# One written-out list of steps for the middle of a decoder block: from the second half of the memory values to the first column group of the up projection

## The chip, the cores and the metric

The kernel runs on one core of one Trainium2 chip. The metric is the device time of one execution in microseconds (us); the runs' median is given. The core has a matrix engine (PE, with its weight loads shown as PEld), a vector engine (DVE), an activation engine (ACT), a general engine (POOL, which also issues DMAs of the software queue) and a sync engine (SP, which here issues plain DMAs). Each engine works through its own instructions in their order and waits for others by semaphores. Matrix products are added up in banks of PSUM and read from there by ACT and DVE.

## The reference, cut to what matters

A decoder block for 1024 tokens of width 1024, all in 32-bit floats. The part that the change touches is everything between the memory attention's softmax and the up projection:

```python
def _memory_cross_attention(h, m, w_q, w_kv, w_o):
    ...
    o = jnp.einsum('bhqk,bhkd->bhqd', p.astype(v.dtype), v)
    return jnp.einsum('bsc,cd->bsd', _merge(o), w_o)
    ...
    x = x + jnp.einsum('bsc,cd->bsd', mixed, w_out[l])
    h = _rmsnorm(x, xattn_norm_g[l])
    m = _rmsnorm(mem, mem_norm_g[l])
    x = x + _memory_cross_attention(h, m, w_mq[l], w_mkv[l], w_mo[l])
    h = _rmsnorm(x, ffn_norm_g[l])
    u = jnp.einsum('bsd,df->bsf', h, w_up[l])
    u = _causal_dwconv(u, conv_w[l], conv_b[l])
    gate, val = jnp.split(u, 2, axis=-1)
    x = x + jnp.einsum('bsf,fd->bsd', jax.nn.silu(gate) * val, w_down[l])
```

Ahead of it stand two kinds of causal self-attention over 8 heads each; behind it the down projection and a last norm. d_ff is 2816, so the up projection has 22 column groups of 128 gate and 128 value columns.

## The kernel before, in words

**Numbers as pairs.** An operand of a product is a pair of a rounded high part and a low part. ACT (sometimes POOL) rounds the high part, DVE subtracts it from the source to get the low part (`split` L204, `split_op` L1127). `mm3` (L199) then makes three matmuls of 128 x 512 for each product of a 128-row tile: high x high (L201), high x low (L202), low x high (L203).

**Products from seven parts.** The memory's output projection ("mo") and the up projection are each computed from 2 x 2 blocks with seven products in place of eight, from sums of blocks. So many sums of operands have to be ready, and each product's result is added to several places. Product 1 of mo is the loop over `pmo` (L1086 to L1103): its first half goes, negated, into `u` (ACT, L1099) and out of the residual `xr` (DVE, L1101). Then come five products by `mo_product` (L1135) in the order 5, 7, 6, 3, 4, each of 4 steps f with 2 splits and 4 x 3 matmuls, which end in 4 banks that `done5` to `done4` (L1150 to L1167) add to `xr` or `u` by DVE. `xr` are 8 tiles of 128 tokens x 1024 columns.

**Sums of the doubled operands.** The second half of the memory values is copied by ACT to `s1` and `s3` and to `a22` and `a22n12` (`evac1`, L1067). The sums that mo's products want are then made by accumulating DMAs of POOL's queue (`onto_a`, L1073): s1 += a22; s3 += high and low of the first half; later s1 += high and low again and s3 += s4. `u` goes into `xr` by 12 more accumulating DMAs of 256 KB, 4 ahead of product 5 and 8 behind product 6 (L1100, L1161). The operand differences of the weights are made by DVE (b11 = b12 - b11, L1115; b22 - b11, L1123) and POOL (b12 - b22, L1116; b21 - b11, L1182).

**Norm and first columns.** `ffn_norm` (L1203) normalises 4 tiles at a time; PE transposes them (`tr`, L1214, bank `ptn`), and `f1` and the pair `b` come from that (L1228 to L1233). For the second 4 tiles the loop at L1347 makes the pairs t1, b22, t2, t3, t4 (tiles `t`, `bt_q`, `bt_k`, `bt_v`). Weights of a column group n are loaded as raw tiles, and `prep_gate`, `prep_sums` and `prep_a22` make its seven operands a11, a12, s1 to s4, a22 (POOL sums L1284 to L1290, splits by ACT or POOL and DVE). Products p1 and p2 of n = 0 and 1 come first, then p5, p6, p7 of column 0 k by k with p4 one behind, then p3 and p4. The loop over the other columns follows, each 7 products of 4 x 3 matmuls, with `cg` and `cv` as sums, the convolution (`conv`, L1386) and the gate. One tile `cg` serves all columns: `first_sum` (L1330) writes it for the next column once the convolution of the last has read it.

**What sets the order.** The two self-attentions and the mixed projection's first half are ordered by `Plan` (L53): a list of `Step`s, each with an engine, a length in ns, the steps that it comes after, named buffers that it takes and gives back, a due time `at`, a time `late` until others see its end, and `lock` (DVE and POOL slow each other while both are in such a step). `run` simulates the engines and returns the steps in their order; they are emitted with the framework's own scheduling switched off. All that follows the mixed projection, the stage of the change included, is ordered by the framework's scheduler. In both cases the framework puts in the waits by what the instructions read and write. The pool `wk` has 4 tiles of 128 x 1024 for normalised rows, softmax rows and operands.

Of the kernel before, what the change touches and what calls it, by code (L numbers as in the profile page):

```python
# [19 lines left out]
P = 128  # L20
D = 1024
# [31 lines left out]
class Plan:  # L53
# [3 lines left out]
    def __init__(self, bufs):  # L57
        self.bufs, self.steps, self.emitted = dict(bufs), [], 0
# [21 lines left out]
    def run(self):  # L80
# [13 lines left out]
        while len(order) < len(left):  # L94
# [39 lines left out]
def hybrid_block(ctx, tc, x, mem, w, wf, pcol, bfg, fing, out):  # L134
# [816 lines left out]
    wk = mid.enter_context(tc.tile_pool(name="wk", bufs=4, reuse_waits="tile"))  # L951
# [67 lines left out]
    def mem_values(probs, evac):  # L1019
        for h in range(4):  # L1020
            pth, ptl = [], []
            for mb in range(2):
                pt = ps.tile([P, 512], F32, tag="T", name="ptm", bufs=2)
                for j in range(4):
                    T.transpose(pt[:, j * P:(j + 1) * P],
                                probs[h][:, j, mb * P:(mb + 1) * P], ident)
                if mb == 0:
                    t = sqp.tile([P, 1024], F32R, tag="sq", name="ptm0")
                    a_, b_ = t[:, :512], t[:, 512:]
                else:  # L1030
                    a_ = wrk.tile([P, 512], F32R, tag="pth1", name="pthm")
                    b_ = wrk.tile([P, 512], F32R, tag="ptl1", name="ptlm")
                split(a_, b_, pt, 1.0)
                pth.append(a_)
                ptl.append(b_)
            for cc in range(2):
                c = 2 * h + cc
                po = ps.tile([P, 512], F32, tag="P", name="pom", bufs=3)
                for mb in range(2):
                    mm3(po, (mv[0][:, mb, c * P:(c + 1) * P], mv[1][:, mb, c * P:(c + 1) * P]),  # L1040
                        (pth[mb], ptl[mb]), mb == 0, mb == 1)
                evac(c, po)
# [7 lines left out]

    probs = mem_probs(0)
    omw = [slot(k, f"om0{n_}").rearrange("p k c -> p (k c)") for k, n_ in ((3, "h"), (0, "l"))]
    om = [[t[:, c * 512:(c + 1) * 512] for c in range(KC)] for t in omw]
    mem_values(probs, lambda c, po: split(om[0][c], om[1][c], po, -1.0))
    probs = mem_probs(1)
    to = ti0 + 8

# [4 lines left out]
    s1t, a22t = [[qkp["f"].tile([P, D], F32, tag=g, name=f"om1{g}{i}") for i in range(2)] for g in ("q", "k1")]  # L1062
    s3t, s4t = [vp.tile([P, 2, 1024], F32, tag="v", name=f"mos{i}") for i in range(2)]
    s3t, s4t = [[t[:, i, :] for i in range(2)] for t in (s3t, s4t)]
    s1, a22, s3, a22n12 = two(s1t), two(a22t), two(s3t), two(s4t)

    def evac1(c, po):  # L1067
        for t in ((s1, s3), (a22, a22n12))[c // 4]:
            A.activation(t[c % 4], po, AF.Copy)

    mem_values(probs, evac1)

    def onto_a(dst, src):  # L1073
        nc.gpsimd.dma_start(dst, src, accum_op=add)

# [4 lines left out]
    for i in range(2):  # L1080
        onto_a(s1t[i], a22t[i])
    for a in range(2):
        for i in range(2):
            onto_a(s3t[i], om_pair(a, 0, i))
    for a in range(2):
        for i in range(2):  # L1086
            onto_a(s4t[i], om_pair(a, 1, i))
    u = vp.tile([P, 2, 1024], F32, tag="v", name="mou")
# [586 lines left out]
```

## Time and profile before

| | us |
|---|---|
| median of 3 runs | 1630.74 |
| lowest and highest run | 1629.62, 1633.43 |
| the profiled execution's own time | 1631.46 |
| its span in the trace | 1629.6 |
| the stage from the second memory values to the end of column group 1 | 177.75 (from 842.00 to 1019.75) |

Rows of windows have: stretch and its length, busy time of PE, PEld, DVE, ACT and POOL with the number of instructions, the clock granted to PE as a share of full speed, the DMA engines' busy share, and GB/s. Rows of groups have: line, engine, operation, output <- inputs, shapes, count | busy time, mean ns of one | idle time of the engine just before. Rows of waits have: who waits <- for what: total, times, longest. Rows of a timeline have: start, time, engine, line and operation, and in brackets the idle time before with what ended it. Rows of DMA issues have: KB of each and median time from issue to landing. A matmul's record is longer than its share of the pace, since matmuls are pipelined.

### The profile page before, as it was taken

To read this page: it belongs to the slowest core of one execution; us is meant where nothing else is said; L and a number is where in the kernel's file an instruction comes from. 1 tells how busy PE (TensorE), PEld (TensorE's weight loads), DVE (VectorE), ACT (ScalarE), POOL (GpSimd) and SP (SyncE) were. 2 spreads that over 40 slices of the span, in tenths; PEclk is the share of its full clock that TensorE was granted. 3 is DMA by queue.
4 is the path that set the end of the run, shared out by engine and by line. 5 is a ranking of instruction groups with operands and counts; after the bars stand their busy time and mean duration, and the time that the engine had idled before them with its cause. 6 is when DMAs were issued, how large, how long until landed. Compare 5 with 4: busy or idle time off the path is not lost. (4 is left out here: it accounts for less than half of the span.)

```text
span 1629.6 us, 22061 instructions
## 1 busy us (share of the span) xinstructions
PE 1547.3 (95%) x7812; PEld 1275.9 (78%) x7812; DVE 1201.1 (74%) x1952; ACT 788.4 (48%) x1546; POOL 540.0 (33%) x534
## 2 busy tenths in 40 slices
PE   7999999999999889999998987999999999999997
PEld 7678887887788767778886765877888888788886
DVE  7377777777867773365544979999999999786566
ACT  7368767767757660034334374333333333445444
POOL 2022313322321210123124439454554444133331
PEclk9999999999999999999999998999999999999999
DMA  5211021011113645512149731222222221998782
GB/s 178 104 53 66 27 65 65 27 53 65 40 53 130 233 142 188 174 45 73 52 139 209 134 119 52 94 87 80 89 78 83 86 91 65 323 296 204 150 189 104
DMA packets 76205, 183.53 MB, mean 113 GB/s; under 512 B 8376, under 2 KB 8504, under 8 KB 75840
## 3 DMA queue, kind: packets, MB, share of 16 engines
q1 hardware_dynamic: 61392, 151.58, 27.1%
q0 software_dynamic: 14400, 30.42, 10.3%
q8 instruction: 61, 1.00, 0.3%
q14 instruction: 48, 0.39, 0.1%
q10 hardware_dynamic: 304, 0.14, 0.0%
HBM read 129.64 MB, written 33.59 MB: 100 GB/s over the span
## 5 line engine op out<-in xcount | busy, mean ns | idle before, releaser
L658 POOL TENSOR_TENSOR p<-p,aw 128x383 f32<-128x383 f32 (+4 forms) x64 | 79.7, 1247 | 182.9 <-DVE aw L652 144.7
L708 DVE TENSOR_TENSOR ptl<-pt,pth 128x512 fp32r<-128x512 f32 x192 | 103.8, 549 | 36.4 <-ACT pth L704 35.0
L202 PE MATMUL dn<-opb,opa 128*128 128x512 f32 x308 | 120.5, 391 | 3.0 <-DVE opb L1133 3.0
L704 ACT ACTIVATE pth<-pt 128x512 fp32r<-128x512 f32 x192 | 92.5, 491 | 60.9 <-PE pt L700 56.9
L203 PE MATMUL dn<-opb,opa 128*128 128x512 f32 x308 | 120.3, 391 | 0.0
L636 POOL TENSOR_SCALAR p<-p,fx 128x128 f32<-128x128 f32 (+3 forms) x64 | 47.9, 753 | 212.1 <-DVE fx L588 166.3
L201 PE MATMUL dn<-opb,opa 128*128 128x512 f32 x308 | 117.9, 391 | 0.0
L700 PE MATMUL pt<-ident,p 128*128 128x128 f32 x576 | 96.6, 277 | 7.2 <-DVE ptl L708 7.1
L1284 POOL TENSOR_TENSOR tmp<-wv 128x512 f32<-128x512 f32 x21 | 43.1, 2050 | 162.6 <-DMA wv<-in_w_dram 153.1
L700 PEld LDWEIGHTS pt<-ident,p 128*128 128x128 f32 x576 | 70.4, 142 | 23.6 <-DVE ptl L708 12.0
L382 DVE TENSOR_TENSOR wlo<-wraw,whi 128x512 fp32r<-128x512 f32 x84 | 66.6, 825 | 24.8 <-ACT whi L377 23.4
L193 POOL TENSOR_SCALAR whi<-wraw 128x512 fp32r<-128x512 f32 x44 | 27.8, 645 | 154.2 <-PE pm L203 62.6
L1388 ACT ACTIVATE yv<-cv,pc 128x1024 f32<-128x1024 f32 x22 | 27.3, 1242 | 101.2 <-DVE cv L1420 93.1
L717 PE MATMUL po<-ptl,v 128*128 128x512 f32 x192 | 69.8, 364 | 5.1 <-DVE ptl L708 4.8
L377 ACT ACTIVATE whi<-wraw 128x512 fp32r<-128x512 f32 x84 | 49.7, 627 | 48.1 <-DMA wraw<-in_w_dram 22.7
L716 PE MATMUL po<-pth,v 128*128 128x512 f32 x192 | 71.1, 370 | 1.7 <-ACT k1f L465 1.5
L201 PE MATMUL up_p<-b,a 128*128 128x512 f32 x176 | 68.4, 392 | 4.1 <-DVE cg L1332 2.7
L202 PEld LDWEIGHTS dn<-opb,opa 128*128 128x128 f32 x308 | 58.2, 189 | 15.6 <-DVE opb L1133 3.5
L202 PE MATMUL up_p<-b,a 128*128 128x512 f32 x176 | 69.0, 392 | 0.0
L203 PE MATMUL up_p<-b,a 128*128 128x512 f32 x176 | 68.7, 391 | 0.0
L201 PEld LDWEIGHTS dn<-opb,opa 128*128 128x128 f32 x308 | 58.1, 189 | 12.1
L203 PEld LDWEIGHTS dn<-opb,opa 128*128 128x128 f32 x308 | 58.2, 189 | 12.0
(504 smaller groups left out, 5234.5 us busy)
## 6 DMA issues: line engine op xcount, KB each, us to landing
wraw<-in_w_dram SPq DMA_DIRECT2D x136, 256.0 KB, 3.0
a_d<-yv SPq DMA_DIRECT2D x22, 512.0 KB, 2.6
wv<-in_w_dram SPq DMA_DIRECT2D x21, 512.0 KB, 3.5
wg<-in_w_dram SPq DMA_DIRECT2D x20, 512.0 KB, 3.4
dn<-a_d POOLq DMA_DIRECT2D x32, 256.0 KB, 6.8
dn<-a_d SPq DMA_DIRECT2D x24, 256.0 KB, 9.8
dn<-in_w_dram SPq DMA_DIRECT2D x24, 256.0 KB, 8.6
xin<-in_x_dram SPq DMA_DIRECT2D x8, 512.0 KB, 5.2
```

The source lines that it names most:

```text
L201: T.matmul(o, lt[0], rt[0], start=start, stop=False)
L202: T.matmul(o, lt[0], rt[1], start=False, stop=False)
L203: T.matmul(o, lt[1], rt[0], start=False, stop=stop)
L377: A.activation(t["hi"][:, c], t["raw", n], AF.Copy)
L382: in_turn("low", lambda: V.tensor_tensor(t["lo"][:, c], t["raw", n], t["hi"][:, c].bitcast(F32), op=ALU.subtract))
L636: G.tensor_scalar(out=c_["p"], in0=c_["p"], scalar1=c_["fx"][:, 3:4], scalar2=0.0, op0=ALU.mult, op1=ALU.add)
L658: G.tensor_tensor(c_["p"][:, :n0 - 1], c_["p"][:, :n0 - 1], c_["a"][:, 1:], op=ALU.mult)
L700: T.transpose(pt[:, j * P:(j + 1) * P], self.rows[j]["p"][:, kb * P:(kb + 1) * P], ident)
L704: A.activation(t[:, 512 - n:], self.sp["pt", kb][:, 512 - n:], AF.Copy)
L708: V.tensor_tensor(t[:, 512 - n:], self.sp["pt", kb][:, 512 - n:], self.sp["th", kb][:, 512 - n:].bitcast(F32), op=ALU.subtract)
L716: T.matmul(self.po[:, c], lv, self.sp["th", kb][:, c], start=kb == 0, stop=False)
L717: T.matmul(self.po[:, c], lv, self.sp["tl", kb][:, c], start=False, stop=kb == 4 * self.g + 3)
```

## The change

A second plan, `mid_plan = Plan({...}, AHEAD=12)`, takes over from the second half of the memory values up to and including all seven products of column group 0 and p1, p2 of group 1. The lengths in it are ROUND = 521 ns (ACT), LOW = 623 ns (DVE), SUM = 1300 ns and STORE = 1050 ns (POOL), and ADD = 6000 ns for the landing of an accumulating DMA. `Plan` gets `ahead`: no step begins more than that many us before its due time, and `late` is not counted between steps of one engine. With it:

- mo's products come in the order 5, 3, 6, 7, 4; those of column 0 as p5, p6, p3, p7, p4.
- s1, s3 and s4's first sums are made by DVE, straight from the bank (`onto_s1`, `plus_high`, `plus_low`), no longer by DMA.
- The first half of product 1 goes only into `u`. `u`, and the results of products 6 and 7, are copied by ACT and added to both halves of `xr` rows by broadcast accumulating DMAs of 512 KB (`both`): the 128 x 512 source is read twice. There are 8 for u, 4 for product 6 and 4 for product 7; with 2 for s4, 4 for s2 and 4 for t3/t4 that makes 26 accumulating DMAs of 512 KB, where there were 12 of 256 KB and 16 of 512 KB.
- b12 - b22 goes from POOL to DVE. t1 and t2 come from the bank in one DVE instruction each, t3 and t4 from an accumulating DMA onto f1, and their low parts go from POOL to DVE.
- There are two tiles `cg`, and `wk` has 7 tiles. The raw value weights of column 1 are loaded into a `wk` tile that the second norm's rows give back after the last transpose.
- The matmuls are the same in number and shape; DVE has 17 instructions more in its list, ACT 12 fewer, POOL 14 fewer.

The diff, cut to its core:

```diff
-    def __init__(self, bufs):
-        self.bufs, self.steps, self.emitted = dict(bufs), [], 0
+    def __init__(self, bufs, ahead=None):
+        self.bufs, self.steps, self.emitted, self.ahead = dict(bufs), [], 0, ahead
...
+                    if self.ahead is not None and now < (s.at - self.ahead) * 1e3:
+                        heappush(events, (s.at - self.ahead) * 1e3)
+                        continue
...
-                            insort(due[f.eng], (f.at, f.seq, max(p.end + p.late for p in f.after), f))
+                            insort(due[f.eng], (f.at, f.seq, max(p.end + p.late * (self.ahead is None or p.eng != f.eng) for p in f.after), f))
...
-    wk = mid.enter_context(tc.tile_pool(name="wk", bufs=4, reuse_waits="tile"))
+    wk = mid.enter_context(tc.tile_pool(name="wk", bufs=7, reuse_waits="tile"))
...
+    mid_plan = Plan({"P": 3, "S": 3, "T": 2, "hi": 0, "lo": 0, "raw": 3, "xn": 3, "m0": 1, "m1": 1, "acc": 3}, AHEAD)
+    on = mid_plan.add
+    MM, ROUND, LOW, SUM, STORE, ADD = 3 * 232, act(512), dve(512), 1300, 1050, 6000
...
-    for i in range(2):
-        onto_a(s1t[i], a22t[i])
...
+                def plus_high(c=c, t=(s3, a22n12)[q][f]):
+                    V.tensor_tensor(t, cell["po", c], om[0][c].bitcast(F32), op=add)
+
+                def plus_low(c=c, t=(s3, a22n12)[q][f]):
+                    V.tensor_tensor(t, t, om[1][c].bitcast(F32), op=add)
+
+                def onto_s1(c=c, t=s1[f]):
+                    V.tensor_tensor(t, cell["po", c], t, op=add)
...
+    def accumulate(name, dst, src, after, at):
+        accs[name] = on(POOL, STORE, lambda: onto_a(dst, src), after, ["acc"], at=at, late=ADD)
+        on(DMA, 0, lambda: None, [accs[name]], [], ["acc"], at=0, late=0)
+        return accs[name]
+
+    def both(dst, src):
+
+        return dst.rearrange("p (h c) -> p h c", h=2), src.unsqueeze(1).broadcast_to([P, 2, 512])
...
-            if s == 0:
-                last_u = A.activation(u[j], pm, AF.Copy, scale=-1.0).ins
-                onto_a(xr[j][:, hi_], u[j])
-            i_ = V.tensor_tensor(xr[j][:, lo_], xr[j][:, lo_], pm, op=sub)
...
+                for h in range(2):
+                    accumulate(("u", h, j), *both(xr[4 * h + j], u[j]), lo_steps[-1:] + [u_steps[j]], 50 + 10 * h)
...
+    o5 = mo_steps(5, s1, b11, [[made["s1", 1, f]] for f in range(4)], [[t_] for t_ in t1s], "PSTP", 31)
+    outs_at = 42.5
+    for j in range(4):
+        outs(5, j, "PSTP"[j], ([j], add_to(xr[j][:, hi_], o5, j)), ([4 + j], add_to(xr[4 + j][:, hi_], o5, j)))
+    for a in range(2):
+        for i in range(2):
+            accumulate(("s2", a, i), s1t[i], om_pair(a, 0, i),
+                       split_steps[5, 0][2 * i:2 * i + 2] + ([accs["s2", 0, i]] if a else []), 39 + a)
...
+    o3 = mo_steps(3, a22n12, b22, [[accs["s4x", f // 2]] for f in range(4)], [[loads[4 + f // 2]] for f in range(4)], "STPS",
+                  42)
...
+            c_.append(on(ACT, ROUND, copy, [split_steps[k, "out"][j]] + split_steps[k, 0], [], ["PSPS"[j]] * (k == 7), at=outs_at))
+            finals[4 + j].append(accumulate((k, j), *both(xr[4 + j], dst[j]), c_[-1:], outs_at + 1))
...
+    g1, v1 = load_steps(1, ([tmps], [last_turn]), ([], ["xn"]), (66, 90))
...
+            cgs[n] = retile(7, "cg1") if n else wk.tile([P, D], F32, tag="xn", name="cg0")
...
+    order = mid_plan.run()
+    with tc.manual_schedule(engines={ENG.PE, ENG.DVE, ENG.Activation, ENG.Pool, ENG.SP}):
+        for f in order:
+            f()
```

How the instructions stand now is shown at three places. The first is DVE at the end of mo's product 5, when its four banks `mo` are added to the halves of `xr`; `moa` and `mob` are the low parts of the two operands of a following product, `mow` raw weights, `mos` and `om1q` raw operands. Before:

```order
L1133 TENSOR_TENSOR moa_9346<-mos0_8902,moa_9346 128x512
L1133 TENSOR_TENSOR mob_9347<-mow_9215,mob_9347 128x512
L1151 TENSOR_TENSOR xr0_7355<-mo_9236,xr0_7355 128x512
L1152 TENSOR_TENSOR xr4_7359<-mo_9236,xr4_7359 128x512
L1133 TENSOR_TENSOR moa_9364<-mos0_8902,moa_9364 128x512
L1133 TENSOR_TENSOR mob_9365<-mow_9215,mob_9365 128x512
L1151 TENSOR_TENSOR xr1_7356<-mo_9237,xr1_7356 128x512
L1152 TENSOR_TENSOR xr5_7360<-mo_9237,xr5_7360 128x512
```

With the change the same place on DVE reads:

```order
L1253 TENSOR_TENSOR mob_9247<-mow01_8929,mob_9247 128x512
L1286 TENSOR_TENSOR xr0_7355<-mo_9252,xr0_7355 128x512
L1286 TENSOR_TENSOR xr4_7359<-mo_9252,xr4_7359 128x512
L1286 TENSOR_TENSOR xr1_7356<-mo_9259,xr1_7356 128x512
L1286 TENSOR_TENSOR xr5_7360<-mo_9259,xr5_7360 128x512
L1286 TENSOR_TENSOR xr2_7357<-mo_9266,xr2_7357 128x512
L1286 TENSOR_TENSOR xr6_7361<-mo_9266,xr6_7361 128x512
L1286 TENSOR_TENSOR xr3_7358<-mo_9273,xr3_7358 128x512
L1286 TENSOR_TENSOR xr7_7362<-mo_9273,xr7_7362 128x512
L1253 TENSOR_TENSOR mob_9322<-mow01_8929,mob_9322 128x512
L1253 TENSOR_TENSOR moa_9384<-mos1_8925,moa_9384 128x512
```

All eight sums of product 5 now stand ahead of the low parts of product 3's third step, which were mixed in between them.

The second place is POOL in the same stretch: accumulating DMAs (`DMA`) and its tensor instructions. `mos` before holds s3 and s4; `mou` is u. `om1q` is s1. Before:

```order
L1074 DMA mos0_8902<-om0l_8293 128x1024
L1074 DMA xr0_7355<-mou_9054 128x512
L1074 DMA xr1_7356<-mou_9054 128x512
L1074 DMA xr2_7357<-mou_9054 128x512
L1074 DMA om1q0_8898<-om1k10_8900 128x1024
L1074 DMA mos1_8903<-om0h_8292 128x1024
L1074 DMA xr3_7358<-mou_9054 128x512
```

With the change, u is `mos2` and the rows of `om1q` are the sums for product 6:

```order
L1081 DMA mos1_8925<-mos0_8924 128x1024
L1081 DMA om1q0_8920<-om0h_8294 128x1024
L1081 DMA om1q0_8920<-om0l_8295 128x1024
L1081 DMA xr0_7355<-mos2_8926 128x2x512
L1081 DMA mos1_8925<-mos0_8924 128x1024
L1229 TENSOR_TENSOR mow10_8930<-mow10_8930,mow_8927 128x512
L1081 DMA om1q1_8921<-om0h_8294 128x1024
L1081 DMA om1q1_8921<-om0l_8295 128x1024
L1229 TENSOR_TENSOR mow10_8930<-mow10_8930,mow_8927 128x512
L1081 DMA xr1_7356<-mos2_8926 128x2x512
```

The DMA that adds u to `xr0` has moved behind two accumulating DMAs onto the same tile `om1q0`, and the one for `xr1` behind two more.

The third place is PE at the end of column group 0: `s11` is the operand s1 of column group 1, so its row is the first of that group's p5. Before:

```order
L202 MATMUL up_p3_10053<-bt_k1_9898,s40_10021 128x512
L203 MATMUL up_p3_10053<-bt_q_9896,s40_10021 128x512
L201 MATMUL up_p6_9926<-t201_9892,ops_9762 128x512
L202 MATMUL up_p7_9930<-bt_v1_9901,ops_9762 128x512
L203 MATMUL up_p7_9930<-bt_v0_9900,ops_9762 128x512
L201 MATMUL up_p5_10168<-t1_9890,s11_10070 128x512
L202 MATMUL up_p5_10168<-t1_9890,s11_10070 128x512
```

With the change (L204 to L206 are the three lines of `mm3` in the changed kernel):

```order
L204 MATMUL up_p3_10001<-bt_q_9922,s40_9834 128x512
L205 MATMUL up_p3_10001<-bt_k1_9924,s40_9834 128x512
L206 MATMUL up_p3_10001<-bt_q_9922,s40_9834 128x512
L204 MATMUL up_p5_10166<-t1_9889,s11_10030 128x512
L205 MATMUL up_p5_10166<-t1_9889,s11_10030 128x512
L204 MATMUL up_p7_10039<-bt_k20_9925,ops_9618 128x512
L205 MATMUL up_p7_10039<-bt_v0_9926,ops_9618 128x512
```

Two matmuls of group 1's p5 now stand ahead of all of p7 and the end of p4 of group 0.

More of the change, by code (lines that the diff above doesn't have):

```diff
@@ L1064, in hybrid_block, with pairs @@
[L1064 to L1071, printed above, removed]
+    def pairs(t):
+        return t[:, :512], t[:, 512:]
     def onto_a(dst, src):
         nc.gpsimd.dma_start(dst, src, accum_op=add)
+    s1t, a22t = [[qkp["f"].tile([P, D], F32, tag=g, name=f"om1{g}{i}") for i in range(2)] for g in ("q", "k1")]
@@ L1245, in hybrid_block @@
[L1245 to L1273 removed]
+        V.tensor_tensor(dst[1], src, dst[0].bitcast(F32), op=sub)
```

707 lines of the change are left out of this document (456 added, 251 removed).

## The prediction

> **What bounds the kernel now.** The page is read first, for the whole and for PE's share:
>
> ```profile
> span 1629.6 us, 22061 instructions
> PE 1547.3 (95%) x7812; PEld 1275.9 (78%) x7812; DVE 1201.1 (74%) x1952; ACT 788.4 (48%) x1546; POOL 540.0 (33%) x534
> ```
>
> PE is busy for 95% of the span, so a change that leaves its matmuls alone can win only where PE stands still or is slowed. The windows show where that is, by stage:
>
> ```profile
> 842.00:881.00 39.00, 37.65 (x191) 30.80 (x190) 18.06 (x28) 20.00 (x43) 13.90 (x15) 1.00 0.79 210
> 881.00:1019.75 138.75, 117.90 (x484) 89.88 (x485) 115.83 (x153) 68.04 (x118) 79.31 (x68) 0.93 0.47 113
> 842.00:1019.75 177.75, 155.55 (x674) 120.68 (x673) 133.89 (x180) 88.04 (x161) 93.20 (x83) 0.94 0.54 134
> 1019.75:1055.00 35.25, 35.25 (x157) 29.21 (x156) 35.08 (x41) 11.69 (x16) 17.14 (x14) 1.00 0.30 99
> 1055.00:1110.00 55.00, 50.93 (x223) 41.23 (x222) 53.39 (x58) 16.67 (x22) 27.61 (x21) 1.00 0.24 82
> 1200.00:1300.00 100.00, 100.00 (x443) 82.81 (x442) 92.86 (x108) 31.46 (x41) 50.02 (x38) 1.00 0.23 79
> ```
>
> The steady loop (the last row) gives PE's pace: 443 matmuls in 100 us, 0.2257 us each. The stage of the change (third row) is PE 155.55 of 177.75 at a clock of 0.94, and DVE 133.89. Its two ends and its transposes in PE's timeline:
>
> ```profile
> 841.89 0.39 PE L203 MATMUL pqm<-h_k,wlo 128*128 128x512 f32 x1
> 851.38 1.03 PE L1025 MATMUL ptm<-ident,pm 128*128 128x128 f32 x8
> 1019.75 0.39 PE L201 MATMUL up_p<-bt_v,a 128*128 128x512 f32 x1
> ```
>
> From the code, the stage holds 552 matmuls of 128x512 (48 of the values, 96 of product 1, 240 of the five products, 168 of two column groups), 24 half as wide and 96 transposes, 672 in all beside the window's 674. A matmul's record is 0.39 - 0.2257 = 0.16 longer than its pace, so eight transposes take (1.03 - 0.16)/8 = 0.108 each. The floor is 552 x 0.2257 + 24 x 0.113 + 96 x 0.108 = 124.6 + 2.7 + 10.4 = 137.7 us. **40.0 us of the stage are not matmul pace.** The longest waits of PE in it, ACT's wait that stands behind the first, and the start of mo's five products:
>
> ```profile
> PE mo L201 <- ACT moa L1130: 5.5, 1, 5.5
> PE up_p L202 <- DVE bt_k L1361: 2.8, 1, 2.8
> PE up_p L202 <- POOL bt_v L1365: 2.8, 1, 2.8
> PE up_p L203 <- DVE ops L1133: 2.6, 1, 2.6
> ACT moa L1130 <- DMA om1q<-om1k: 15.5, 2, 11.4
> ```
>
> ```profile
> 889.35 2.07 PE L201 MATMUL mo<-mob,moa 128*128 128x512 f32 x4 [5.46 <-ACT moa L1130]
> ```
>
> The first mo product, at 47.35 of the stage (last row), waits for s1, which waits for its accumulating DMA; the others wait for operands that DVE and POOL make one after the other. The rest of the 40 is smaller waits and a slow clock behind each wait:
>
> ```profile
> 1010.04 0.39 PE L203 MATMUL up_p<-t4x,ops 128*128 128x512 f32 x1
> 1013.04 0.79 PE L203 MATMUL up_p<-t,ops 128*128 128x512 f32 x1 [2.62 <-DVE ops L1133]
> ...
> 1016.20 0.51 PE L201 MATMUL up_p<-t,ops 128*128 128x512 f32 x1
> ```
>
> Between the last two rows stand seven intervals, 3.16 us, where the pace gives 1.58: a wait of 2.62 cost 1.58 more, 0.6 us for each us waited.
>
> **The change part by part.** The matmuls stay. I lay them out at their pace, 0 being 842.00, with the new order, and ask what is late.
>
> Doubled sums on DVE. The s1, s3 and s4 sums leave the DMA queue for 16 DVE instructions. Two DVE instructions of this shape in a row take 1.28 (below), or 0.61 each with the tail, so 9.7 us more on DVE, mostly while it is idle: in the first window it is busy 18.06 of 39.
>
> ```profile
> 888.37 1.28 DVE L1133 TENSOR_TENSOR mob<-mow,mob 128x512 fp32r<-128x512 f32 x2
> L1133 DVE TENSOR_TENSOR mob<-mow,mob 128x512 fp32r<-128x512 f32 x20 | 14.6, 735 | 0.0
> L1133 DVE TENSOR_TENSOR ops<-wv,ops 128x512 fp32r<-128x512 f32 x2 | 2.9, 1430 | 0.0
> L1133 DVE TENSOR_TENSOR a<-wg,a 128x512 fp32r<-128x512 f32 x3 | 3.6, 1208 | 0.0
> L1130 ACT ACTIVATE mob<-mow 128x512 fp32r<-128x512 f32 x20 | 12.1, 615 | 0.0
> L1116 POOL TENSOR_TENSOR mow<-mow,mow 128x512 f32<-128x512 f32 x4 | 5.8, 1458 | 4.0 <-DVE mow L1115 4.0
> ```
>
> The first mo matmul can then start with PE's own work done: 2.7 + 32 transposes 3.5 + 48 and 96 matmuls 32.5 = 38.7. The 5.5 goes.
>
> Sums by DMA. What these DMAs take now, and how fast the queue is when it is full:
>
> ```profile
> 884.00:902.00 18.00, 12.34 (x45) 9.73 (x46) 12.19 (x15) 7.31 (x14) 13.01 (x13) 0.81 1.05 206
> xr<-mou POOLq DMA_DIRECT2D x12, 256.0 KB, 4.9
> om1q<-om0h POOLq DMA_DIRECT2D x2, 512.0 KB, 7.0
> om1q<-om0l POOLq DMA_DIRECT2D x2, 512.0 KB, 6.3
> mos<-mos POOLq DMA_DIRECT2D x2, 512.0 KB, 5.5
> tmp<-in_w_dram SPq DMA_DIRECT2D x2, 256.0 KB, 6.6
> raw_g<-in_w_dram SPq DMA_DIRECT2D x2, 256.0 KB, 4.6
> ```
>
> On POOL the DMA of u into `xr0` now stands behind two accumulates onto one tile (the order above). The first needs the low parts of product 5's first steps, at about 39.4; the second waits for its landing, 7.0 later, and u is issued behind it at about 47.4 and lands, at 5.5, near 53. DVE's sum of product 5 into `xr0` writes the same tile and has to wait for that, and behind it in DVE's queue stand ten instructions up to the low part that product 3's third step reads: 53 + 10 x 0.61 = 59, where PE would want it at 38.7 + 48 x 0.2257 + 24 x 0.2257 = 55.0. **(a) 3.7 to 4, taken as 3.7.** The plan's steps have no such relation between u and that sum, so it is not planned for. **(b)** The same for `xr1` to `xr3` and product 3's sums, from u's DMAs landing one after the other: 1.5. Both are nothing if the queue lands in 4 us, and twice that if it takes 7. No broadcast accumulate is in the trace: below, it costs what 512 KB costs at 206 GB/s, 2.5 of transfer; above, twice the landing of 256 KB, 9.8. I take 5.5, the row of an accumulate of 512 KB from SBUF.
>
> By the Trainium skill (DMA: Bandwidth & Descriptors, "Anatomy of one DMA"), a DMA of this path takes 2.0 us and its bytes at 436 GB/s, an estimate of 3.2 for 512 KB. The rows of 5.5 to 7.0 disagree, all from a busy queue. By that figure (a), (b) and the slow clock behind (a) would be gone, and the forecast 7.4 lower.
>
> Product order and lows. (c) Product 7's first operands stand behind product 6's sums on DVE: 7 rows, about 1.8 late. (d) Two matmuls of group 1's p5 stand ahead of p7 of group 0 on PE (the order above), and want the sum s1 of raw weights that can be loaded only after the last transpose: load 5.6 (between 4.6 and 6.6), POOL's sum 1.46, rounding 0.62, 7.7 in all, under which lie 18 matmuls, 4.1. So **3.6**. (e) The slow clock behind (a) and (d): 0.6 x 7.3 = 4.4. (f) DVE beside POOL's tensor instructions takes 1.43 or 1.21 where it takes 0.73 elsewhere; 16 of POOL's leave for DVE or DMA, but the weight sums stay, beside the t parts. I take 8 of DVE's on the path, 0.6 each: 4.8. (g) Small starts, as the trace has now: 2.
>
> Sum of what stays: 3.7 + 1.5 + 1.8 + 3.6 + 4.4 + 4.8 + 2 = 21.8; the stage is 137.7 + 21.8 = 159.5, **18.2 less** than 177.75.
>
> Two cg tiles, seven wk tiles. The loop's waits after the stage, and one at the memory norm:
>
> ```profile
> 1060.26 0.50 PE L201 MATMUL up_p<-b,a 128*128 128x512 f32 x1 [1.36 <-ACT cg L1331]
> 1082.87 0.47 PE L201 MATMUL up_p<-b,a 128*128 128x512 f32 x1 [1.44 <-DVE cg L1332]
> 1103.46 0.47 PE L201 MATMUL up_p<-b,a 128*128 128x512 f32 x1 [1.27 <-DVE cg L1332]
> 710.99 0.66 PE L233 MATMUL ptn<-ident,xn 128*128 128x128 f32 x4 [1.56 <-DVE h_0l L211]
> ```
>
> With a second cg the first three, 4.07 in all, need not come; but DVE is full there (53.39 of 55), so between 0 and 4.1; I take **2**. The norm's rows of the second half find free tiles earlier, and their transposes can fill the last: 0 to 1.56, taken **1.5**.
>
> The total is 18.2 + 2 + 1.5 = 21.7. The profiled execution itself took 1631.46 (span 1629.6), the median is 1630.74, 0.7 less. 1631.46 - 21.7 - 0.7 = 1609.1: **1609**. Its own range, with (a) to (d) from half to one and a half times, the loop from 0 to 4 and (f) from 2 to 8: 1600 to 1618.
>
> At one place a page would alter a term: the Trainium skill (TensorE: Matmul & The Clock Gate, "What's actually happening") has the clock halved only after an idle window of about 3.4 us. The trace has it after 2.62, so the measurement decides. By the page (d) might cost no clock, and the forecast would be 2 lower.
>
> **The rivals.** *The waits for DMA vanish.* If the queue is calm without the s1 and s3 sums, landings stay near 4 us; (a), (b), their part of (e), 2.3, and (f), with 16 POOL instructions gone, fall away: 21.8 - 3.7 - 1.5 - 2.3 - 4.8 = 9.5. With the loop's 4.1: 40.0 - 9.5 + 4.1 + 1.5 = 36.1, so 1595. For it: 206 GB/s and landings of 7.0 come from one burst. Against: u's chain of three is still one behind the other.
>
> *DVE becomes the bound.* From 881 on DVE is idle 22.9. That stretch gets 18.2 less the 8.4 won ahead of mo (47.35 now, 39 then) = 9.8 shorter, and DVE gets up to 9.7 more to do: 3.4 are left, and every us that DVE waits at (a) or for ACT is lost. Then the waits that were taken off come back as waits for low parts, about 10, and the loop gives nothing: 1621. Against: many of the added sums come early.
>
> *The broadcast accumulates are slow* (the other side). Sixteen of them, and two more s2, run from about 47. If each holds the queue for r us, the last ends at 52 + 16 r. The second norm needs it near 110: five products, 48 matmuls of p1 and p2 and 32 transposes end at 107, plus (a) to (c), less the norm's own 4. Up to r = 3.6 it is hidden; each tenth beyond costs 1.6 us, and from r = 5.0 the gain is spent. At 6, the landings of 5.5 to 7.0 with none beside another: 52 + 96 - 110 = 38 late, 1609 + 38 = 1647. For it: each reads its source twice. Against: the 206 GB/s, which is 2.5 us for 512 KB with several under way.
>
> *The order changes little* because the planner's lengths (521 for 615, 623 for 735) mislead it and new waits of the old size come: 1630.
>
> **How the numbers follow.** Forecast 0.55; waits vanish 0.17; DVE bound 0.18; slow accumulates 0.06; nothing changed 0.04. The range from 1592 to 1625 holds the first three with their margins, and leaves out the last two and the far ends, some 0.15. A measurement here tells 0.2%, 3.3 us, from no change. Faster 0.90, same 0.04, slower 0.06.
>
> **What would show it.** Right: the first mo matmul 38 to 41 us after the last `pqm`; one wait of 3 to 5 us in product 3 with DVE's sum into `xr0` held by a DMA; one of 3 to 4 in p5 of group 1; the stage at 155 to 165. Wrong: waits of PE for the second norm's rows (slow accumulates); DVE over 95% busy from 881 on (DVE bound); the stage under 150 (waits vanish); the loop after the stage longer than now.

## The result, and the profile after

The changed kernel takes 1653.9 us (median of 4 runs, 1651.44 to 1655.7) beside 1630.48 for the kernel before (4 runs): a ratio of the means of 1.0139, with a 95% interval from 1.0123 to 1.0155. **It is 1.4% slower; 1609 was forecast, and the range ended at 1625.** The profiled execution took 1651.44, and its page begins so:

```profile
span 1649.6 us, 21993 instructions
PE 1551.9 (94%) x7812; PEld 1279.4 (78%) x7812; DVE 1206.7 (73%) x1969; ACT 784.9 (48%) x1534; POOL 511.4 (31%) x520
```

The matmuls are the same 7812; 20 us of span were added, and PE's busy time grew by 4.6. The windows of the changed kernel (columns as before) say where:

```profile
881.00:961.00 80.00, 51.05 (x191) 39.78 (x190) 43.69 (x68) 24.13 (x45) 25.46 (x23) 0.81 0.72 155
840.50:1037.70 197.20, 154.85 (x674) 122.85 (x673) 132.18 (x195) 82.61 (x149) 69.14 (x67) 0.90 0.55 135
1220.00:1320.00 100.00, 100.00 (x439) 81.99 (x438) 96.17 (x108) 31.96 (x41) 47.47 (x38) 1.00 0.24 81
```

The stage has grown from 177.8 to 197.2 us for the same 674 instructions, at a clock of 0.90 where it was 0.94. In the 80 us from the first mo matmul on no engine is full: PE is busy for 51 us, DVE for 44, ACT for 24, POOL for 25. So PE's waits there are not for an engine that has too much to do. PE's timeline has the marks and the large waits:

```profile
840.14 0.40 PE L206 MATMUL pqm<-h_k,wlo 128*128 128x512 f32 x1
...
881.46 0.40 PE L204 MATMUL mo<-mob,moa 128*128 128x512 f32 x1
...
901.95 0.79 PE L204 MATMUL mo<-mob,moa 128*128 128x512 f32 x1 [3.97 <-ACT moa L1250]
904.11 0.80 PE L205 MATMUL mo<-mob,moa 128*128 128x512 f32 x1 [1.37 <-DVE mob L1253]
919.91 0.79 PE L205 MATMUL mo<-mob,moa 128*128 128x512 f32 x1 [5.54 <-DVE mob L1253]
954.46 0.79 PE L205 MATMUL mo<-mob,moa 128*128 128x512 f32 x1 [17.79 <-DVE mob L1253]
...
1037.68 0.39 PE L204 MATMUL up_p<-b,a 128*128 128x512 f32 x1
```

The start is as forecast: the first mo matmul comes 41.3 us after the last `pqm` (47.5 before). Then PE waits 28.7 us in the five products, 17.8 of them once. Three of the four large waits are for a low part, which is one instruction of DVE; DVE's timeline shows that DVE itself stood:

```profile
898.58 4.88 DVE L1286 TENSOR_TENSOR xr<-mo,xr 128x512 f32<-128x512 f32 x8 [7.12 <-DMA xr<-mos]
...
916.57 0.69 DVE L1286 TENSOR_TENSOR xr<-xr,mo 128x512 f32<-128x512 f32 x1 [4.45 <-DMA xr<-mos]
...
952.99 0.75 DVE L1388 TENSOR_SCALAR xn<-xr,rs 128x1024 f32<-128x1024 f32 x1 [18.45 <-POOL rs L1385]
```

The first two rows are the waits that the prediction named in (a) and (b): sums into `xr` behind the landing of u. They stand ahead of PE's waits of 1.37 and 5.54. The 3.97 has another cause: PE waits there for a high part, and ACT, which makes it, waited for the landing of s4's sum:

```profile
901.27 1.67 ACT L1250 ACTIVATE moa<-mos 128x512 fp32r<-128x512 f32 x3 [3.14 <-DMA mos<-mos]
```

POOL issued that accumulating DMA at 896.10, behind u's first broadcast at 891.90. The third row of DVE is new: the scaling of a row of the first norm waits 18.45 us for POOL's power, an instruction of about 1 us. POOL's timeline says why:

```profile
921.98 1.22 POOL L1081 DMA_DIRECT2D xr<-mos  x1 [2.68 <-issue]
927.13 1.21 POOL L1081 DMA_DIRECT2D xr<-mos  x1 [3.93 <-issue]
932.25 1.22 POOL L1081 DMA_DIRECT2D xr<-mos  x1 [3.91 <-issue]
940.81 1.21 POOL L1081 DMA_DIRECT2D xr<-mos  x1 [7.34 <-issue]
945.98 1.22 POOL L1081 DMA_DIRECT2D xr<-om1q  x1 [3.96 <-issue]
951.15 1.21 POOL L1081 DMA_DIRECT2D xr<-om1q  x1 [3.95 <-issue]
951.90 1.06 POOL L1385 TENSOR_TENSOR rs<-rs,mhalf 128x1 f32<-128x1 f32 x1
```

The broadcast accumulates are issued 5.15 us apart, once 8.56. In between POOL does nothing for 3.9 us and waits, by the profile, for nothing ("issue"): the next issue is held. The trace's landings say until when: the DMA of 927.13 lands at 931.93 and the next is issued at 932.25; that one takes 8.24 us to land in place of 4.8, and the next is issued 0.3 us after it. So only one broadcast is under way at a time. The power stands in POOL's queue behind all of these. DVE stands behind the power, and product 7's low part behind that. All of PE's larger waits in the stage, grouped:

```profile
PE mo L205 <- DVE mob L1253: 25.0, 4, 17.8
PE ptn L1401 <- ACT f L1415: 6.4, 2, 5.6
PE mo L204 <- ACT moa L1250: 4.0, 1, 4.0
PE ptn L1401 <- DVE xn L1388: 3.7, 2, 2.8
PE up_p L204 <- ACT s L1546: 2.2, 1, 2.2
```

They were 21.8 us before and are 42.3 now, with three small ones that are not shown.

### The profile page after: what moved, and what is told of

Its sections match the earlier page's. It is cut to its first block, busy times and chain, and to the rows that moved or that the text cites. A ratio compares the mean times of both kernels' runs of the same rounds, so it can differ in the third digit from the quotient of the medians.

```text
span 1649.6 us, 21993 instructions
## 1 busy us (share of the span) xinstructions
PE 1551.9 (94%) x7812; PEld 1279.4 (78%) x7812; DVE 1206.7 (73%) x1969; ACT 784.9 (48%) x1534; POOL 511.4 (31%) x520
## 4 chain that ended last, share of the span: by engine, by line
PE 70%; DVE 9%; issue 9%; ACT 5%; DMA 4%; POOL 3%; POOLq 0%; SPq 0%; DVEq 0%; ACTq 0%
PE up_p L204 6%; PE up_p L206 6%; PE up_p L205 6%; PE dn L205 4%; PE dn L206 4%; PE dn L204 4%; PE pt L703 3%; PE pq L204 3%; PE pq L205 3%; PE pq L206 3%; DMA wraw<-in_w_dram 2%; PE po L720 2%; PE pqm L206 2%; PE po L719 2%; PE pqm L205 2%
## 5 line engine op out<-in xcount | busy, mean ns | idle before, releaser
L206 PE MATMUL dn<-opb,opa 128*128 128x512 f32 x308 | 120.8, 392 | 0.0
L204 PE MATMUL dn<-opb,opa 128*128 128x512 f32 x308 | 118.7, 390 | 0.0
L1491 POOL TENSOR_TENSOR tmp<-wv 128x512 f32<-128x512 f32 x20 | 34.0, 1701 | 165.8 <-DMA wv<-in_w_dram 165.8
L204 PE MATMUL up_p<-b,a 128*128 128x512 f32 x176 | 68.8, 391 | 0.0
L206 PE MATMUL up_p<-b,a 128*128 128x512 f32 x176 | 68.5, 389 | 0.0
L206 PEld LDWEIGHTS dn<-opb,opa 128*128 128x128 f32 x308 | 58.2, 189 | 12.2
L204 PEld LDWEIGHTS dn<-opb,opa 128*128 128x128 f32 x308 | 58.0, 188 | 12.2
```

The source lines that it names most:

```text
L204: T.matmul(o, lt[0], rt[0], start=start, stop=False)
L206: T.matmul(o, lt[1], rt[0], start=False, stop=stop)
```

## The experiments

"Stage" below is the time from the last `pqm` matmul to the 169th of the up projection in the profiled execution; it was 177.9 before and 197.5 after. Each ratio is to runs of the kernel before that were taken beside it.

| kernel | ratio to before, 95% | stage, us |
|---|---|---|
| the change | 1.0139 (1.0123 to 1.0155) | 197.5 |
| pairs for broadcasts | 0.9955 (0.994 to 0.997) | 171.1 |
| twice the descriptor space | 0.9894 (0.9877 to 0.991) | 162.3 |
| kernel before, twice the space | 0.9988 (0.9976 to 1.0) | 178.4 |
| twice the space, u late | 0.9992 (0.9977 to 1.0007) | 174.3 |
| twice the space, u early | 0.9907 (0.9884 to 0.993) | 162.5 |
| pairs, u early | 0.9945 (0.9922 to 0.9968) | 167.5 |
| u early, 1024 bytes | 1.0063 (1.0043 to 1.0082) | 186.6 |
| no power in the first norm | 1.014 (1.0109 to 1.017) | 198.9 |
| planner told the broadcast's price | 1.0201 (1.0181 to 1.0221) | 207.0 |
| twice the space, one cg | 0.9937 (0.9917 to 0.9958) | |
| twice the space, u early, one cg | 0.9935 (0.991 to 0.996) | |
| kernel before, seven wk tiles and two cg | 1.0024 (1.0013 to 1.0034) | 172.8 |

**What holds the issue.** A broadcast accumulate moves 256 rows of 2 KB; the accumulates of before had 128 rows each. Two theories: the queue holds only so many rows' descriptors, or reading one source twice is slow. Four runs tell them apart. First, each broadcast as two plain accumulates, everything else in place:

```diff
+        def issue():
+            if len(dst.shape) == 3:
+                for h in range(2):
+                    onto_a(dst[:, h, :], src[:, h, :])
+            else:
+                onto_a(dst, src)
-        accs[name] = on(POOL, STORE, lambda: onto_a(dst, src), after, ["acc"], at=at, late=ADD)
+        accs[name] = on(POOL, STORE, issue, after, ["acc"], at=at, late=ADD)
```

> Each broadcast accumulate of 512 KB is issued as two plain accumulates of 256 KB, one for each half of the row tile; the order of everything else stays. Theory 1 (the queue holds a limited number of row descriptors, and one broadcast of 256 rows of 2 KB fills it, so POOL stands at the next one until the first has drained): a pair is issued every 2.5 to 3.2 us in place of 5.15, the 17.8 us wait of PE in mo's product 7 shrinks to under 4, the stage falls from 197 to 160 to 170 us and the time to 1615 to 1630. Theory 2 (reading the source twice and adding is what is slow, whatever the form): a pair takes 5 us as before and the time stays at 1650 to 1656. Theory 3 (the order on DVE alone, sums of product 5 behind the landing of u): pairs may be faster, but DVE still waits about 7 us at the sum into xr0 and the time falls by less than 8, to 1645 or above.

It measured 0.9955, 1627.38 us, with the stage at 171.1. The pairs on POOL:

```profile
924.26 0.86 POOL L1081 DMA_DIRECT2D xr<-mos  x1 [0.70 <-issue]
925.76 0.89 POOL L1081 DMA_DIRECT2D xr<-mos  x1 [0.63 <-issue]
927.06 0.87 POOL L1081 DMA_DIRECT2D xr<-mos  x1 [0.42 <-issue]
```

One every 1.3 to 1.5 us, 2.9 for a pair where the broadcast took 5.15, with the same bytes, the same source read twice and the same order. The 17.8 us wait is gone (the largest in that place is 2.2), and the stage is a little above the 160 to 170 of theory 1. Second, the changed kernel with more space:

```diff
-    nc = _bacc.Bacc("TRN2", target_bir_lowering=False, num_devices=1, dynamic_dma_scratch_size=1024)
+    nc = _bacc.Bacc("TRN2", target_bir_lowering=False, num_devices=1, dynamic_dma_scratch_size=2048)
...
-            t = self.sp["tl", kb] = sw.tile([P, 512], F32R, tag="ptl", name="ptl", bufs=NT)
+            t = self.sp["tl", kb] = sw.tile([P, 512], F32R, tag="ptl", name="ptl", bufs=NT - 1)
```

> The changed kernel with twice the descriptor space of the software queue (2048 in place of 1024 bytes per partition); to make room for it one buffer of low softmax parts is taken from the attention ahead (3 in place of 4), which may cost some us before the stage. Theory 1: the broadcasts are issued every 2.6 to 3.5 us in place of 5.15 and the stage falls below 175 us from 197. Theory 2: the pitch of 5.15 stays and so does the stage.

0.9894, 1617.01 us: with one number and one buffer altered, the change is 1.1% faster than the kernel before. Its stage, the middle of it, and PE's largest waits:

```profile
844.50:1006.50 162.00, 146.25 (x673) 116.35 (x672) 133.01 (x195) 82.13 (x148) 70.08 (x67) 0.97 0.67 164
890.00:960.00 70.00, 58.78 (x257) 46.08 (x256) 58.52 (x84) 36.08 (x65) 39.22 (x35) 0.93 0.98 206
```

```profile
PE mo L204 <- ACT moa L1250: 4.5, 1, 4.5
PE mo L205 <- DVE mob L1253: 2.7, 2, 1.6
PE up_p L204 <- ACT s L1546: 2.1, 1, 2.1
PE mo L206 <- DVE moa L1253: 1.7, 1, 1.7
```

Over the same 70 us the changed kernel with 1024 bytes has

```profile
890.00:960.00 70.00, 41.05 (x148) 31.55 (x147) 34.09 (x51) 19.22 (x36) 24.60 (x22) 0.78 0.68 144
```

The DMA engines go from 68% busy and 144 GB/s to 98% and 206: with 1024 bytes they were idle a third of the time while POOL waited to hand them work. Third and fourth, the DMAs alone: eight each of six forms with nothing beside them, in two sizes of space.

```diff
+        for i in range(8):
+            G.dma_start(flat[i], long[i % 2][:, :1024], accum_op=add)
+        rest()
+        for i in range(8):
+            G.dma_start(dst[i], long[i % 2][:, :512].unsqueeze(1).broadcast_to([P, 2, 512]), accum_op=add)
+        rest()
+        for i in range(8):
+            G.dma_start(dst[i], srcs[i % 2][:, :, :512], accum_op=add)
```

> A kernel that does nothing of the block: eight accumulating DMAs on-chip of each of six forms, with nothing beside them, with 1024 bytes of descriptor space. Theory 1: time from one issue to the next goes by the rows: 128 rows of 2 KB (256 KB) about 1.3 to 1.6 us, 128 rows of 4 KB (512 KB) about 2.6, broadcast 256 rows of 2 KB about 5, the same 512 KB from two different source halves also about 5, broadcast of 256 rows of 1 KB (256 KB) well over twice the 128 rows of 2 KB, and 64 partitions of broadcast (128 rows, 256 KB) about 1.5. Theory 2: forms that read the source twice are slow, the one with two source halves is as fast as 128 rows of 4 KB.

> The same six forms with 4096 bytes of descriptor space. Theory 1: the broadcast forms come down to the time of 512 KB in 128 rows, about 2.6 us from issue to issue. Theory 2: they stay near 5 us.

POOL with 1024 bytes, one row of each form as it repeats; busy and idle time together are the step from issue to issue. L72 is 128 rows of 2 KB, L75 128 rows of 4 KB, L78 the broadcast, L81 the same with two source halves, L84 256 rows of 1 KB:

```profile
18.62 0.86 POOL L72 DMA_DIRECT2D dst<-src  x1 [0.55 <-issue]
...
37.15 0.86 POOL L75 DMA_DIRECT2D dst<-src  x1 [1.86 <-issue]
...
56.02 1.20 POOL L78 DMA_DIRECT2D dst<-src  x1 [4.13 <-issue]
...
98.75 1.20 POOL L81 DMA_DIRECT2D dst<-src  x1 [4.12 <-issue]
...
138.92 1.21 POOL L84 DMA_DIRECT2D dst<-src  x1 [2.88 <-issue]
```

512 KB take 2.7 in 128 rows and 5.3 in 256, whether the source is read twice or not; 256 KB take 1.4 to 1.6 in 128 rows and 4.1 in 256. By the landings, each broadcast is again issued 0.3 us after the one before it has landed. With 4096 bytes, rows of L72 and of the broadcast:

```profile
11.91 7.22 POOL L72 DMA_DIRECT2D dst<-src  x8 [11.46 <-DVE src L55]
...
37.55 4.86 POOL L78 DMA_DIRECT2D dst<-src  x4 [7.41 <-DVE dst L66]
48.65 4.87 POOL L78 DMA_DIRECT2D dst<-src  x4 [6.24 <-DVE dst L66]
```

Now four broadcasts go out in a row, and from the first of them to the fifth it is 11.1 us, 2.8 each. By the landings one is done every 2.7 to 3.1 us, where 512 KB in 128 rows take 2.5 to 3.0. So with 1024 bytes the rows decide, and more space takes their price away: that is shown for DMAs over 128 partitions. One expectation missed: 64 partitions of broadcast, 128 rows, step at 2.7 and not 1.5 (177.53 to 180.27). With 4096 bytes the first of them land 2.8 us apart too, so it is not the space that sets this form's step; what does stays open.

The Trainium skill (DMA: Bandwidth & Descriptors, "SWDGE vs HWDGE vs iDMA") has the software queue's descriptors written to rings in a part of SBUF. The runs agree, if `dynamic_dma_scratch_size` is the size of that part: it sets the step, 5.3 us at 1024 and 2.8 at 4096.

**Whether the space itself is the gain.** The kernel before with the same two edits:

> The kernel before with 2048 bytes of descriptor space and three buffers of low softmax parts in place of four: what the descriptor space gives to it. If the space helps only the broadcasts of 256 rows: the stage from the second memory values stays at 175 to 178 us, and the time is within 0.2% of before or slower by what the missing buffer costs. If the queue was full before too (DMAs of 128 rows were issued 1.3 to 1.6 us apart): the stage falls by up to 5 us, since the s1 sum that the first mo product waits for lands earlier.

0.9988, the stage 178.4: in the kernel before, whose accumulates have 128 rows, the space gives next to nothing. It pays in the order with broadcasts. There the stage falls by 35.2 us with 2048 bytes; pairs at 1024 bytes win 26.4 of them; what the other 8.8 hang on stays open.

**By which way it costs.** POOL's power of the first norm is left out, so its rows are scaled by the mean square:

```diff
-                G.tensor_tensor(rs[:, j:j + 1], rs[:, j:j + 1], mhalf[:, :1], op=ALU.pow)
+                if th:
+                    G.tensor_tensor(rs[:, j:j + 1], rs[:, j:j + 1], mhalf[:, :1], op=ALU.pow)
```

> The changed kernel (1024 bytes), in which POOL's power of the first norm's four row scales is left out, so its rows are scaled by the mean square itself; all else stays in place. Way 1 (POOL stands at the issue of broadcasts, and the powers wait behind them): DVE's scaling no longer waits 18.5 us for POOL, the wait of 17.8 us in product 7 goes to under 4, and the stage falls from 197 to 178 to 188 us. Way 3 (the last broadcasts land too late for the second norm anyway): the 17.8 us go, but PE then waits as long for the second norm's rows, and the stage stays at 193 to 198.

1.014, the stage 198.9. The 17.8 us in product 7 went to 0.9, and in their place, on PE, stands

```profile
PE ptn L1402 <- DVE xn L1389: 18.9, 1, 18.9
```

Way 1 is out, since the stage did not fall; way 3 had the size, but looked for the wait at the second norm. DVE's scaling of the first norm's last row stands behind a weight operand, and that behind ACT:

```profile
965.26 0.63 ACT L1547 ACTIVATE ops<-tmp 128x512 fp32r<-128x512 f32 x1 [19.69 <-POOL tmp L1563]
```

It is POOL again: with the power gone, the next POOL instruction behind the broadcasts, a weight sum, holds ACT, then DVE, then PE. So the power was only the first in the line. Next, u into `xr0` to `xr3` is due earlier, with 1024 bytes:

```diff
-                    accumulate(("u", h, j), *both(xr[4 * h + j], u[j]), lo_steps[-1:] + [u_steps[j]], 50 + 10 * h)
+                    accumulate(("u", h, j), *both(xr[4 * h + j], u[j]), lo_steps[-1:] + [u_steps[j]], 30 + 30 * h)
```

> The changed kernel (1024 bytes) with u's four DMAs into xr0 to xr3 due at 30 in place of 50, ahead of the s2 sums. Way 2 (DVE held by u's landing at the sums of products 5 and 3: waits of PE of 4.0, 1.4 and 5.5): they shrink to under 4 together, and the stage falls from 197 by 6 to 12 us. Way 3: the queue only starts its 82 us of broadcasts earlier, by about 10 us, and the second half lands earlier by the same; then the 17.8 us wait shrinks too, and the stage falls by 10 to 18.

1.0063, the stage 186.6, 10.9 less: the first broadcast is issued 26.4 us after the last `pqm` in place of 51.8. But the wait at product 3 is 7.1 (ACT's high part again, behind the landing of s4's sum at 907.11), and one of 18.1 stays; neither theory had both. And the planner, told the price:

```diff
-        accs[name] = on(POOL, STORE, lambda: onto_a(dst, src), after, ["acc"], at=at, late=ADD)
+        accs[name] = on(POOL, 4000 if len(dst.shape) == 3 else STORE, lambda: onto_a(dst, src), after, ["acc"], at=at,
+                        late=1000 if len(dst.shape) == 3 else ADD)
```

> The changed kernel, with 1024 bytes of descriptor space, whose planner is told that a broadcast accumulate holds POOL for 4000 ns and lands 1000 later, where it was told 1050 and 6000; the order that it makes puts three of the first norm's four powers on POOL ahead of product 6's broadcasts. Theory 1 (the 17.8 us wait is POOL's queue: the norm's powers stand behind broadcasts that each hold POOL for 5.15 us): that wait goes, and the time falls from 1.4% above before to between 0.4% below and 0.5% above. Rival (the landing of all the broadcasts is what is too late, whatever stands behind them): the total of the queue, 16 x 5.15, stays on the path, PE waits for the second norm's rows instead, and the time stays at 1.0 to 1.5% above.

1.0201, the stage 207.0, slower than either theory allowed. Three powers now stand ahead of product 6's broadcasts, the fourth still behind all four of them:

```profile
967.48 1.33 PE L1402 MATMUL ptn<-ident,xn 128*128 128x128 f32 x5 [10.91 <-DVE xn L1389]
```

So no order of this list that was tried hides sixteen holds of POOL; only shortening them did.

**DVE behind u's landing** (step a of the prediction), with 2048 bytes: u's DMAs behind the sums of product 3, or early as in the diff above.

```diff
-                for h in range(2):
-                    accumulate(("u", h, j), *both(xr[4 * h + j], u[j]), lo_steps[-1:] + [u_steps[j]], 50 + 10 * h)
...
-        outs(3, j, "STPS"[j], ([j], add_to(xr[j][:, hi_], o3, j, sub, True)))
+        o_ = outs(3, j, "STPS"[j], ([j], add_to(xr[j][:, hi_], o3, j, sub, True)))
+        for h in range(2):
+            accumulate(("u", h, j), *both(xr[4 * h + j], u[j]), [lo_steps[j], u_steps[j]] + o_, 54 + 10 * h)
```

> The changed kernel with 2048 bytes of descriptor space (and three buffers of low softmax parts), and with u's eight accumulating DMAs put behind the sums of mo's product 3, so that no sum of products 5 and 3 into xr stands on DVE behind the landing of u. Theory A (the prediction's step a: DVE held by u's landing, with low parts of product 3 queued behind): the waits of PE of 4.5, 1.6 and 1.7 us at product 3's third step shrink to under 2 together, and the time falls by 5 to 9 us against the run with 2048 bytes alone, to a ratio of 0.983 to 0.987 to before. Theory B (those waits come from the sum s2 and the s4 sum that are needed there anyway): they stay, and the ratio stays at 0.988 to 0.991; u's later landing may then hold the norm's rows and cost up to 3 us.

> The changed kernel with 2048 bytes of descriptor space (three buffers of low softmax parts), and the due time of u's four accumulating DMAs into xr0 to xr3 moved from 50 to 30, so that POOL issues them ahead of the s2 sums (u into xr4 to xr7 stays at 60). Theory A (step a of the prediction: DVE's sum of product 5 into xr0 stands behind u's landing; put later, u only came late at the end of the chain): the waits of 4.5, 1.6 and 1.7 us at product 3's third step go or shrink to under 2 together, nothing comes late behind, and the ratio to before falls from 0.989 to 0.983 to 0.987. Theory B (the early u holds the queue when the s4 and s2 sums want it): product 3 or 6 waits for its operand instead, and the ratio is 0.988 to 0.995.

> With 1024 bytes as in the change itself: each broadcast as two accumulates of 256 KB, and u into xr0 to xr3 due at 30 in place of 50. Against the pairs alone (0.9955), theory A gives 5 to 9 us less, 0.990 to 0.993. Theory B gives 0.994 to 0.998.

Late: the three waits of 4.5, 1.6 and 1.7 us fell to 1.4 and 0.8, nearly as theory A had it, but the stage is 12 us longer than with u at its old place, and the ratio, 0.9992 beside 0.9894, lies outside both ranges: later waits come for the copies of product 7, for norm rows and for operands of the up projection, the longest

```profile
941.68 0.80 PE L204 MATMUL mo<-mob,moa 128*128 128x512 f32 x1 [5.67 <-ACT mos L1317]
```

Early: those waits fell to 3.0 and 0.5, with new ones of 1.6 at product 6 and 2.3 at the transposes; the stage is 162.5 for 162.3 and the ratio 0.9907 for 0.9894, the same within the intervals. With pairs, 0.9945 for 0.9955, also the same; there a wait in product 7 grew from 2.2 to 8.2. Theory B holds: what (a) costs is taken by the next in the queue when it goes. The run with u early and 2048 bytes also says which of product 3's waits are (a)'s:

```profile
892.01 4.87 DVE L1286 TENSOR_TENSOR xr<-mo,xr 128x512 f32<-128x512 f32 x8
...
900.44 1.15 ACT L1250 ACTIVATE moa<-mos 128x512 fp32r<-128x512 f32 x2 [1.32 <-DMA mos<-mos]
```

DVE's eight sums are not held by u any more, and yet PE waits 3.0 us for ACT's high part, which waits for s4's sum. That sum lands 61.6 us after the last `pqm` with u at its old place, 59.6 with u early and 57.9 with u late, and the wait is 4.5, 3.0 and 1.4. So the largest of the three waits depends on when s4's DMA gets through POOL's queue, and not on DVE.

**Two tiles cg.** One tile, with 2048 bytes:

```diff
         x_ = [part_steps(n, "p1", "a11", "b11", "P", [b_steps[kc] for kc in range(4)], 85 + 5.6 * n),
...
+        if n:
+            continue
...
-        cg = cgs[n % 2]
+        cg = cgs[0]
...
-            first_sum(n, cg)
         if n > 0:
+            first_sum(n, cg)
             product(n, "p6", "s2", t2, "P")
```

> The changed kernel with 2048 bytes of descriptor space (three buffers of low softmax parts) and one tile cg for all columns, as before: the sum of column 1's first two products moves back into the loop. By the prediction two tiles gain 2 us, so this would be 2 us slower, 0.9905. By the rival (DVE is full in the loop, and running ahead only makes PE wait for cv): the loop from the 169th up matmul to its end is 1 to 3 us shorter than 388 us and the ratio 0.987 to 0.989.

> Both edits together, u early and one tile cg, with 2048 bytes: the sum of the two effects if they are independent, which I expect at 0.982 to 0.987; if u early only shifts the wait, 0.987 to 0.990.

0.9937, and 0.9935 with u early: slower than expected both times, the second outside both of its ranges. From the last `pqm` to the first down-projection matmul the trace has 554.9 us with one tile and 550.6 with two: **two tiles gain 4.3** (6.5 with u early), and the rival falls. But only 1.1 of the 4.3 are in the loop behind the 169th matmul (389.3 for 388.3). There the waits for cg, 3.2 us with one tile, are gone with two, and waits of 3.3 for cv stand in their place; a wait of 1.3 for a weight sum is gone too. The other 3.2 are ahead of it, and their cause stays open. The other way round, two tiles and seven wk tiles given to the kernel before:

```diff
-    wk = mid.enter_context(tc.tile_pool(name="wk", bufs=4, reuse_waits="tile"))
+    wk = mid.enter_context(tc.tile_pool(name="wk", bufs=7, reuse_waits="tile"))
...
-    cg = retile(7, "cg")
+    cgs = [retile(7, "cg"), wk.tile([P, D], F32, tag="xn", name="cg1")]
...
+        cg = cgs[n % 2]
```

> The kernel before with seven wk tiles and two tiles cg in turn, nothing else of the change. By the prediction: the three loop waits of 1.36, 1.44 and 1.27 us go (0 to 4.1, taken as 2), and the wait of 1.56 us at the memory norm goes (1.5): together 3.5 us, a ratio of 0.998. Rival (DVE is full in the loop, so a second cg only moves the waits, and the changed kernel's loop, 2.5 us longer, shows it): the loop stays the same or up to 2.5 us longer, the norm gains 1.5, and the ratio is 0.999 to 1.001.

1.0024, slower, and outside both ranges. The stage is 5 us shorter, and the loop behind it 9 longer; PE waits there are now

```profile
PE up_p L201 <- DVE cv L1414: 9.5, 3, 4.4
```

where they were 4.07 for cg. The wait at the memory norm is not touched by seven tiles (it was 1.56):

```profile
712.62 0.66 PE L233 MATMUL ptn<-ident,xn 128*128 128x128 f32 x4 [1.60 <-DVE h_0l L211]
```

The version that beats both kernels is the change with 2048 bytes, 0.9894.

## Why the prediction was wrong, point by point

- **What bounds the kernel: right.** 40 us of the stage were not matmul pace. With the broadcasts' step cut, the changed order has the stage at 162.3; the sum gave 159.5. That they are so near is in part luck: there the start was 2.6 later than in the sum and the waits at (a) and (b) 2.6 larger, (d) was 1.5 smaller, and (c), (f) and (g) were not measured.
- **Doubled sums on DVE: right in kind.** The first mo matmul came at 41.3 in place of 38.7; the 5.5 us wait went, 6.2 were won and not 8.4.
- **Sums by DMA: the step that failed.** It priced the broadcast as "the row of an accumulate of 512 KB from SBUF", 5.5 to landing. That held (4.8), but it is not what the DMA costs the kernel. The rows were all of 128-row DMAs, of which several were under way at once, hence 206 GB/s; the 256-row form is one at a time at 1024 bytes, 5.15 a piece, and POOL stands for it. The rival of slow accumulates had the price right ("from r = 5.0 the gain is spent") and was argued down by the 206 GB/s, a rate of another form. At r = 5.15 its own formula gives 52 + 82 - 110 = 24 us late, so 1633. The other 20 are put down to what the formula left out, the instructions queued on POOL behind the issues; no run measures them by themselves. The rival's place was off too: the largest wait came in product 7, through the first norm's power, and not at the second norm. The prediction counted for each DMA when it lands and not how long it holds its queue.
- **(a) and (b): the place right, the cause in part, the size not.** PE's waits there came to 3.97 + 1.37 + 5.54 = 10.9, where 5.2 stood in the sum; with 2048 bytes 7.8. DVE behind u's landing is behind the 1.37 and the 5.54. The 3.97 is for s4's sum, late in POOL's queue, which (a) did not count; that it fell into the 3 to 5 us named as a sign is luck. That removing them gains anything was not borne out.
- **(d): right in place, too large.** Group 1's p5 waited 2.2 (for ACT's `s`), 3.6 in the sum.
- **(e), the slow clock.** PE's waits in the stage add up to 42.3 and the rest over the floor is 197.5 - 137.7 - 42.3 = 17.5. With (c) and (f) in it, that is at most 0.4 for each us waited; 0.6, from one wait, was taken. (c), (f) and (g) were not tried by themselves.
- **Two cg: 2 taken, 4.3 measured** in the changed kernel with 2048 bytes, 1.1 of it in the loop that the prediction had in mind, and a loss in the kernel before. From the 169th matmul to the end of the loop the change still takes 388.3 us for 385.7. That is one thing: 439 matmuls in 100 us of the steady loop where there were 443, also with one cg (439 or 440), and 443 in the kernel before with two. Why some 50 of them take 0.24 us in place of 0.2257 was not found; it stays open.
- **Seven wk tiles: 1.5 taken, nothing found** at the memory norm in the kernel before.
- **The page's figure.** The fit of the Trainium skill (DMA: Bandwidth & Descriptors, "Anatomy of one DMA"), by which I estimate 3.2 us for 512 KB, would have put the forecast further off; the measurement decides, 4.8 to landing and 5.15 from issue to issue at 1024 bytes.

## What to carry to other kernels

Price a DMA of the software queue by how long it holds the engine that issues it, in the form (rows, not bytes) that will run: with 1024 bytes one of 256 rows is not two of 128. Where a change lengthens an engine's holds, look for small instructions of that engine on which others wait; they move with it, and taking away the first only shows the next. A rate measured on a full queue says nothing of a form that cannot fill it.

## What the runs showed of the hardware

An accumulating DMA of 256 rows steps at 5.3 us with 1024 bytes of descriptor space and at 2.8 with 4096, for 512 KB; at 4.1 for 256 KB with 1024. In 128 rows it is 2.7 and 1.4 to 1.6, with 1024. With 1024 bytes a 256-row DMA of 512 KB is issued only 0.3 us after the one before it has landed. The wait has no name in the profile: POOL's idle time reads "issue". And 1024 bytes more of descriptor space were worth 35 us of stage to one order of the work and nothing to the other (177.9 and 178.4).
